# Row tiles in pairs, shifted copies on ScalarE, modulation sums later and a rank for the first row tile, in a two-layer hybrid mixer

## The chip, the cores and the metric

The kernel runs on one core of a Trainium2 chip. The metric is the device time of one execution in microseconds. Before the change it was run three times: 1634.55, 1635.33 and 1639.21 us, median 1635.33.

## What is computed

Two layers, each made of a SwiGLU feed-forward part, a token mixer and a second feed-forward part. Each part gets its input scaled and shifted by a modulation that is formed from a vector `c`, and ends in a residual sum and a layer norm. All data are float32; there are 256 tokens of 1024 channels.

```python
mod = (silu(c) @ ada_w[l] + ada_b[l]).reshape(3, 3, 1, D_MODEL)      # D_MODEL = 1024
u = modulate(h, mod[0, 0], mod[0, 1])
h = layer_norm(ALPHA * h + 0.5 * mod[0, 2] * swiglu_ffn(u, ...), ...)
u = modulate(h, mod[1, 0], mod[1, 1])
h = layer_norm(ALPHA * h + mod[1, 2] * hybrid_token_mixer(u, ...), ...)
u = modulate(h, mod[2, 0], mod[2, 1])
h = layer_norm(ALPHA * h + 0.5 * mod[2, 2] * swiglu_ffn(u, ...), ...)

def hybrid_token_mixer(u, ...):
    a_in, b_in, c_in, g_in = split(u @ w_in)
    y_a = silu(layer_norm(causal_dwconv(val * sigmoid(gate), width=31))) @ w_a_out
    y_b = rms_norm((ssd(silu(causal_dwconv(xbc, width=4))) + d * x) * silu(z)) @ w_b_out
    y_c = sparse_attention(c_in) @ w_c_out      # with compressed keys from overlapping blocks of 32
    g = sigmoid(g_in)
    return (g[0] * y_a + g[1] * y_b + g[2] * y_c) @ w_o
```

## The kernel before

**Layout.** Channels lie on the 128 partitions, so the 1024 channels are eight row tiles of 128 partitions x 256 tokens. All weights are cut into blocks of 128x128 and laid out in memory in the order in which they are used; eight blocks make a unit of 512 KB (`unit`, line 535). A unit is loaded into `raw`, ScalarE rounds it to the reduced precision of the fast matmul (`whi`), VectorE forms the rest (`wlo`), and each product is three matmuls: high by high, low by high, high by low (`triple`, lines 577 to 579; `pair` and `single`, lines 593 and 602). One weight tile is three matmuls of 256 columns.

**Order.** The program does not run as it is written. Every instruction is recorded with an engine, an estimated cost, its reads and writes, and a key (`rec`), and `schedule` (line 238) then lays all of them out: at each step, on each engine, the instruction that can start earliest by its estimate goes first; among equal starts the one with the lower key. The key is the number of the weight tile at which the step was recorded, unless `at(...)` or `key=` sets another: taps of the 31-wide convolution get keys spread between the tile of their input and a tile 670 after the start of `mix_a`; the halves of a weight unit get the unit's first tile less 20; a key under -9000 (`RUSH` is 20000) lets an engine wait for that step. TensorE and table-bound activations don't run more than 45 tiles ahead (`AHEAD`); VectorE isn't limited. The result is a fixed order for each engine, which the chip then runs with semaphores. SP issues all DMAs in one such order.

**Buffers.** The planner also gives out buffers. Eleven big ones of 8 KB per partition (`big8`) hold `uh`, `ul`, `ha`, `ca`, `mg`, `zs`, the gates, and each 1 MB block of modulation weights (`ada_raw`); they are given out in the order in which they are first used in the recorded program, first in first out. The 12 temporaries of 128x256 (`t256`, `TMP`), four 128x512 buffers (`pt`, shared by rope, attention and the exponentials of `ssd`) and six PSUM banks (`x_bank`) go to whoever comes first. Two PSUM banks (`mm_bank`) take turns under the weight products.

**Modulation sums.** `ada(l, t0, key)` loads two rows of 128 outputs (1 MB, issued with a key 30 tiles less) and forms each with one VectorE instruction over 1024 elements that multiplies by `sc` and accumulates; a small addition of the bias follows. In layer 0's mixer eight such steps are recorded by `side(i)` in five places, with `COUNT[i]` steps in the i-th; layer 1's mixer has none. Their results are read by `part_begin`, after the fourth row tile of `mix_out`, for the feed-forward part that follows.

**The mixer** (`mixer`, line 958), in recorded order, with the number of weight tiles: `early` (32), `mix_v` (32), `mix_small` (8), `mix_a` (96; input of the long convolution), `mix_c` (128; compression in `windows` and `compress`, rope, queries), gates `g2` (64), `mix_x` (128; short convolution), `attend` (beside the two before), `merge(0)` (64), `side(0)`, `mix_z` (64), `side(1)`, gates `g1` (64), `side(2)`, `ssd` (beside the two before) and `merge(1)` (64), `side(3)`, gates `g0` (64), `conv_end` (beside), `side(4)`, `merge(2)` (64), `mix_out` (64).

**At the start** the first feed-forward part takes its eight row tiles as they come: for each, `ready(k)` (in `start`, line 1558) issues the next loads, forms the modulation, `A`, and by `u_tile` the high part `uh`, a copy `u` and the low part `ul`.

Of the kernel before, what the change touches and what calls it, by code (L numbers as in the profile page):

```python
# [14 lines left out]
ALU = mybir.AluOpType  # L15
# [3 lines left out]
P = 128  # L19
# [333 lines left out]
COUNT = (2, 2, 2, 2, 0)  # L353
# [9 lines left out]
class Net(Plan):  # L363
    BIG = 11
    TMP = 12
# [60 lines left out]
    def x_bank(self, name="x", kind="misc"):  # L426
        return self.buf(self.pools["x"], "x", (P, 512), F32, name, kind=kind, psum=True)

# [670 lines left out]
    def windows(self, m, which):  # L1099
# [5 lines left out]
        for g in range(2):  # L1105
            r = slice(g * 64, g * 64 + 64)
            self.act(Sg[0:64, :, g, :], mv[r], AF.Copy)
            self.cp(Sg[64:, :, g, 0:T - 1], mv[r, :, 1:])
# [254 lines left out]
    def conv_end(self):  # L1363
# [12 lines left out]
        for e in range(KT):  # L1376
            with self.at(pos - TAIL[0] + TAIL[1] * e):
                self.tt(r[:, e], r[:, e], mean, ALU.subtract)
                sq.append(self.t256("sq"))
                self.act(sq[e], r[:, e], AF.Square)  # L1380
                if e % 4 == 3:
                    self.partial(var, sq[e - 3:], e > 3)
# [20 lines left out]
    def mix_x(self):  # L1403
# [9 lines left out]
        for i in range(16):  # L1413
# [7 lines left out]
            acc = self.t256("acc")  # L1421
# [7 lines left out]
            if i < 8:  # L1429
                tb = self.x_bank("xt")  # L1430
                for t in range(2):
                    self.trans(tb[:, t * P:t * P + P], o[:, t * P:t * P + P], self.c("ident"))
                for t in range(2):
                    self.tt(self.xdt[:, t, i * P:i * P + P].rearrange("p (h c) -> p h c", h=2),
                            tb[:, t * P:t * P + P].rearrange("p (h c) -> p h c", h=2),
                            self.smt[:, t, 64 + 2 * i:66 + 2 * i][:, :, None].to_broadcast([P, 2, 64]), ALU.mult)
            elif i >= 12:
                g = i - 12
                cb = self.x_bank("cb")
                self.mm(cb[:, :T], bc[:, g, :P], bc[:, 4 + g], True, True)  # L1440
                self.mm(cb[:, T:384], bc[:, g, P:], bc[:, 4 + g, P:], True, True)
                t = one((P, 384), f"cbt{g}")
                self.act(t, cb[:, :384], AF.Copy)
                self.cbt[g] = t

    def mix_z(self):
        self.zs = self.big8("zs")
        for i in range(0, KT, 2):
# [3 lines left out]
            for j in range(2):  # L1452
                zz = self.t256("zz")
                self.act(zz, m[:, j * T:j * T + T], AF.Copy, scale=0.5)
                th = self.t256("th")
                self.act(th, zz, AF.Tanh)
                self.stt(self.zs[:, i + j], th, 1.0, zz, ALU.add, ALU.mult)

    def ssd(self):
# [5 lines left out]
        for h in range(1, HEADS, 2):  # L1465
            with self.at(self.ssd0 + MARGIN[3] + (h - 1) * span / HEADS):
# [52 lines left out]
    def merge(self, step, yh, yl, rs=None, th=None):  # L1519
# [8 lines left out]
        for d in range(0, KT, 2):  # L1528
# [3 lines left out]
            for j in range(2):  # L1532
                y = m[:, j * T:j * T + T]
                t = gates[:, d + j]
                g = self.mg[:, d + j]
                if step == 0:
                    self.stt(g, t, 1.0, y, ALU.add, ALU.mult)
                    continue
                self.stt(t, t, 1.0, y, ALU.add, ALU.mult)
                if rs is not None:  # L1540
# [218 lines left out]
```

## Time and profile before

| | |
|---|---|
| median of three runs | 1635.33 us |
| profiled execution | 1632.52 us, its span 1630.7 us |
| TensorE busy, share of the span | 1580.8 us, 97% |
| weight loads | 1503.3 us, 92% |
| VectorE | 1381.3 us, 85% |
| ScalarE | 980.0 us, 60% |
| TensorE's mean granted clock | 0.995 |
| DMA, mean | 216 GB/s |
| TensorE in the chain that ended last | 84% |

The span is the time between the first and the last instruction of one execution. A busy engine isn't always the one that others wait for: the shares are means over stages. What a wait costs is read from TensorE's idle time and from what ended it.

### The profile page before, as it was taken

To read this page: it belongs to the slowest core of one execution; us is meant where nothing else is said; L and a number is where in the kernel's file an instruction comes from. 1 tells how busy PE (TensorE), PEld (TensorE's weight loads), DVE (VectorE), ACT (ScalarE), POOL (GpSimd) and SP (SyncE) were. 2 spreads that over 40 slices of the span, in tenths; PEclk is the share of its full clock that TensorE was granted. 3 is DMA by queue.
4 is the path that set the end of the run, shared out by engine and by line. 5 is a ranking of instruction groups with operands and counts; after the bars stand their busy time and mean duration, and the time that the engine had idled before them with its cause. 6 is when DMAs were issued, how large, how long until landed. Compare 5 with 4: busy or idle time off the path is not lost.

```text
span 1630.7 us, 33331 instructions
## 1 busy us (share of the span) xinstructions
PE 1580.8 (97%) x13228; PEld 1503.3 (92%) x13228; DVE 1381.3 (85%) x2676; ACT 980.0 (60%) x1810; POOL 8.3 (1%) x64
## 2 busy tenths in 40 slices
PE   7999999999999999999999999998999999999997
PEld 7999989889988888999989999998998898989996
DVE  7889789999999986899678885999999998776655
ACT  4644585588647466644475445845895567575443
POOL 0000000000000000000000000000000000000000
PEclk9999999999999999999999999999999999999998
DMA  9999665543276555899768885645332545657661
GB/s 372 320 342 396 226 215 180 176 130 98 92 279 214 173 175 187 300 346 364 253 234 294 320 302 174 230 161 173 124 109 92 178 154 161 194 191 241 222 197 42
DMA packets 89886, 351.86 MB, mean 216 GB/s; under 512 B 10369, under 2 KB 13697, under 8 KB 80130
## 3 DMA queue, kind: packets, MB, share of 16 engines
q1 hardware_dynamic: 89730, 349.73, 62.0%
q8 instruction: 104, 1.70, 0.4%
q14 instruction: 52, 0.43, 0.1%
HBM read 343.34 MB, written 1.05 MB: 211 GB/s over the span
## 4 chain that ended last, share of the span: by engine, by line
PE 84%; DVE 8%; DMA 3%; ACT 2%; issue 1%; SPq 0%; ACTq 0%; DVEq 0%
PE mm L577 15%; PE mm L578 15%; PE mm L579 15%; PE mm L455 3%; PE a L455 3%; PE a L593 2%; DMA ada<-in_ada 2%; PE g L577 2%; DVE wlo L474 2%; PE g L578 2%; PE g L579 2%; PE xb L577 2%; PE xb L578 2%; PE xb L579 2%; PE sb L1082 2%
## 5 line engine op out<-in xcount | busy, mean ns | idle before, releaser
L511 ACT ACTIVATE whi<-raw 128x1024 fp32r<-128x1024 f32 x470 | 496.8, 1059 | 315.9 <-PE mm L579 147.8
L474 DVE TENSOR_TENSOR wlo<-raw,whi 128x1024 fp32r<-128x1024 f32 x470 | 573.8, 1223 | 132.8 <-ACT whi L511 131.7
L577 PE MATMUL mm<-uh,whi 128*128 128x256 f32 x1392 | 384.8, 276 | 0.9 <-DVE h L474 0.9
L579 PE MATMUL mm<-ul,whi 128*128 128x256 f32 x1392 | 384.2, 276 | 0.0
L578 PE MATMUL mm<-uh,wlo 128*128 128x256 f32 x1392 | 384.2, 276 | 0.0
L577 PEld LDWEIGHTS mm<-uh,whi 128*128 128x128 f32 x1392 | 261.3, 188 | 2.5 <-ACT uh L511 1.2
L578 PEld LDWEIGHTS mm<-uh,wlo 128*128 128x128 f32 x1392 | 261.3, 188 | 0.1
L579 PEld LDWEIGHTS mm<-ul,whi 128*128 128x128 f32 x1392 | 261.3, 188 | 0.0
L577 PE MATMUL mm<-hh,whi 128*128 128x256 f32 x704 | 195.5, 278 | 0.0
L579 PE MATMUL mm<-hl,whi 128*128 128x256 f32 x704 | 194.7, 277 | 0.0
L578 PE MATMUL mm<-hh,wlo 128*128 128x256 f32 x704 | 194.7, 276 | 0.0
L493 DVE SCALAR_TENSOR_TENSOR ada<-ada,sc 128x1024 f32<-128x1024 f32 x144 | 173.7, 1223 | 24.8 <-DMA ada<-in_ada 19.3
L577 PEld LDWEIGHTS mm<-hh,whi 128*128 128x128 f32 x704 | 132.1, 188 | 1.3 <-issue 1.2
L579 PEld LDWEIGHTS mm<-hl,whi 128*128 128x128 f32 x704 | 132.3, 188 | 0.0
L578 PEld LDWEIGHTS mm<-hh,wlo 128*128 128x128 f32 x704 | 132.2, 188 | 0.1
L578 PE MATMUL g<-uh,wlo 128*128 128x256 f32 x384 | 108.2, 282 | 9.5 <-DVE wlo L474 9.5
L493 DVE SCALAR_TENSOR_TENSOR ca<-ap,vec,ca 128x256 f32<-128x256 f32 x240 | 115.1, 481 | 0.1
L577 PE MATMUL g<-uh,whi 128*128 128x256 f32 x384 | 113.8, 296 | 0.6 <-DVE g L493 0.6
L493 DVE SCALAR_TENSOR_TENSOR acc<-ap,vec,acc 128x256 f32<-128x256 f32 x224 | 108.1, 483 | 0.2
L579 PE MATMUL g<-ul,whi 128*128 128x256 f32 x384 | 107.3, 280 | 0.0
L511 ACT ACTIVATE sg<-mm 128x256 f32<-128x256 f32 x76 | 28.9, 381 | 91.8 <-PE mm L579 91.3
L578 PEld LDWEIGHTS g<-uh,wlo 128*128 128x128 f32 x384 | 73.0, 190 | 11.4 <-DVE wlo L474 11.2
(346 smaller groups left out, 3588.1 us busy)
## 6 DMA issues: line engine op xcount, KB each, us to landing
raw<-in_ws SPq DMA_DIRECT2D x498, 512.0 KB, 4.3
ada<-in_ada SPq DMA_DIRECT2D x71, 1024.0 KB, 8.0
w<-in_w SPq DMA_DIRECT2D x4, 1024.0 KB, 8.3
pt<-q SPq DMA_DIRECT2D x16, 128.0 KB, 5.0
ada<-in_ada SPq DMA_DIRECT2D x2, 512.0 KB, 4.6
x<-in_x SPq DMA_DIRECT2D x8, 128.0 KB, 10.8
pt<-kr SPq DMA_DIRECT2D x8, 128.0 KB, 2.2
kh<-kh SPq DMA_DIRECT2D x4, 256.0 KB, 4.3
```

Source lines behind the costliest of these rows:

```text
L455: return self.op("PE", cost, lambda: self.nc.tensor.matmul(real(out), lhsT=real(lhsT), rhs=real(rhs), start=start, stop=stop), [out], [lhs ...
L474: lambda: self.nc.vector.tensor_tensor(real(out), real(a), real(b), op), [out], [a, b], key)
L493: self.nc.vector.scalar_tensor_tensor(real(out), real(a), real(s), real(b), op0, op1, **k)
L511: self.nc.scalar.activation(real(out), real(a), f, **k)
L577: mm(o, lhsT=a, rhs=c, start=start, stop=False)
L578: mm(o, lhsT=b, rhs=c, start=False, stop=False)
L579: mm(o, lhsT=a, rhs=d, start=False, stop=stop)
L593: self.nc.tensor.matmul(o, lhsT=lhsT, rhs=rhs, start=first, stop=False)
L1082: self.nc.tensor.matmul(real(out), lhsT=real(lhsT), rhs=real(rhs), start=start, stop=stop)
```

## The change

1. `mix_x`, `mix_z`, `ssd`, `merge` and `conv_end` treat two row tiles in one instruction where they had one each (Tanh, the multiplications behind it, the gate products, the squares, the mean subtraction). In `mix_x` the taps of the short convolution accumulate straight in `xs` or `bc`. A single `th2` takes the place of temporaries for Tanh, the squares of a pair use the four `pt` buffers, and the temporaries go from 12 to 10.
2. In `windows` the two copies shifted by one token move from VectorE to ScalarE.
3. `COUNT` goes from (2, 2, 2, 2, 0) to (1, 1, 1, 2, 3).
4. In `start` the steps of row tile 0 get the key -20000 instead of -100.

```diff
-COUNT = (2, 2, 2, 2, 0)
+COUNT = (1, 1, 1, 2, 3)
-    TMP = 12
+    TMP = 10
+    def pair256(self, name):
+        return self.some((P, 512), "pt", 4).rearrange("p (a b) -> p a b", a=2)
+    def twice(self, v):
+        return v[:, None, :].to_broadcast([P, 2, T])
@@ windows
-            self.cp(Sg[64:, :, g, 0:T - 1], mv[r, :, 1:])
+            self.act(Sg[64:, :, g, 0:T - 1], mv[r, :, 1:], AF.Copy)
@@ conv_end
-        for e in range(KT):
-            with self.at(pos - TAIL[0] + TAIL[1] * e):
-                self.tt(r[:, e], r[:, e], mean, ALU.subtract)
-                sq.append(self.t256("sq"))
-                self.act(sq[e], r[:, e], AF.Square)
-                if e % 4 == 3:
-                    self.partial(var, sq[e - 3:], e > 3)
+        for e in range(0, KT, 2):
+            with self.at(pos - TAIL[0] + TAIL[1] * (e + 0.5)):
+                two = r[:, e:e + 2]
+                self.tt(two, two, self.twice(mean), ALU.subtract)
+                q = self.pair256("sq")
+                self.act(q, two, AF.Square)
+                sq += [q[:, 0], q[:, 1]]
+                if e % 4 == 2:
+                    self.partial(var, sq[e - 2:], e > 3)
@@ mix_x
-            acc = self.t256("acc")
+            o = self.xs[:, i] if i < 8 else bc[:, i - 8]
+            acc = o
...
-            th = self.t256("th")
-            self.act(th, acc, AF.Tanh)
-            o = self.xs[:, i] if i < 8 else bc[:, i - 8]
-            self.stt(o, th, 1.0, acc, ALU.add, ALU.mult)
+            if i % 2 == 0:
+                continue
+            th = self.one((P, 2, T), "th2")
+            both = self.xs[:, i - 1:i + 1] if i < 8 else bc[:, i - 9:i - 7]
+            self.act(th, both, AF.Tanh)
+            self.stt(both, th, 1.0, both, ALU.add, ALU.mult)
+            for i, o in ((i - 1, both[:, 0]), (i, both[:, 1])):
...
@@ mix_z
-            for j in range(2):
-                zz = self.t256("zz")
-                self.act(zz, m[:, j * T:j * T + T], AF.Copy, scale=0.5)
-                th = self.t256("th")
-                self.act(th, zz, AF.Tanh)
-                self.stt(self.zs[:, i + j], th, 1.0, zz, ALU.add, ALU.mult)
+            z = self.zs[:, i:i + 2]
+            self.act(z, m.rearrange("p (a b) -> p a b", a=2), AF.Copy, scale=0.5)
+            th = self.one((P, 2, T), "th2")
+            self.act(th, z, AF.Tanh)
+            self.stt(z, th, 1.0, z, ALU.add, ALU.mult)
@@ ssd
-                self.tt(x, x, self.zs[:, i], ALU.mult)
+                if i % 2 == 0:
+                    continue
+                x = self.xs[:, i - 1:i + 1]
+                self.tt(x, x, self.zs[:, i - 1:i + 1], ALU.mult)
                 if i % 4 == 3:
-                    sq = [self.t256("sq") for _ in range(4)]
-                    for g in range(4):
-                        self.act(sq[g], self.xs[:, i - 3 + g], AF.Square)
+                    sq = []
+                    for g in (i - 3, i - 1):
+                        q = self.pair256("sq")
+                        self.act(q, self.xs[:, g:g + 2], AF.Square)
+                        sq += [q[:, 0], q[:, 1]]
@@ merge (the loop over j is gone; y, t, g are pairs)
+            y = m.rearrange("p (a b) -> p a b", a=2)
+            two = slice(d, d + 2)
+            t, g = gates[:, two], self.mg[:, two]
...
+                self.tt(t, t, self.twice(rs), ALU.mult)
@@ start
-            self.ada(0, 8 + k, -100 + k, k, raws[k])
-            self.ts(A[:, k:k + 1], self.mod[0][:, 8 + k:9 + k], 1.0, None, ALU.add, key=-100 + k)
-            with self.at(-100 + k):
+            key = -100 + k if k else -RUSH
+            self.ada(0, 8 + k, key, k, raws[k])
+            self.ts(A[:, k:k + 1], self.mod[0][:, 8 + k:9 + k], 1.0, None, ALU.add, key=key)
+            with self.at(key):
```

## Rows read from the trace of the kernel before

**Rows 1.** The page, busy us (share of the span) xinstructions of each engine.

```profile
PE 1580.8 (97%) x13228; PEld 1503.3 (92%) x13228; DVE 1381.3 (85%) x2676; ACT 980.0 (60%) x1810; POOL 8.3 (1%) x64
```

**Rows 2.** Busy time by stage, layer 0's mixer: stretch, length, busy us of each engine.

```profile
213.34:433.70 220.36, 212.51 (x1810) 200.87 (x1811) 209.41 (x447) 163.85 (x376) 2.88 (x19) 1.00 0.47 154
...
525.00:551.00 26.00, 23.44 (x204) 22.34 (x200) 26.00 (x54) 10.45 (x12) 0.00 (x0) 1.00 0.59 203
551.00:580.00 29.00, 26.91 (x227) 23.72 (x227) 28.54 (x58) 20.73 (x34) 0.12 (x1) 1.00 0.53 170
580.00:607.00 27.00, 25.33 (x194) 24.55 (x195) 22.23 (x45) 16.79 (x32) 0.00 (x0) 0.94 0.53 170
```

**Rows 3.** The same for layer 1's mixer (PE, PEld, DVE, ACT, POOL; clock, DMA).

```profile
1021.64:1242.90 221.26, 214.03 (x1810) 202.46 (x1811) 209.42 (x447) 163.76 (x376) 2.17 (x13) 0.99 0.47 153
...
1334.20:1356.20 22.00, 22.00 (x198) 22.00 (x195) 18.27 (x30) 10.50 (x12) 0.00 (x0) 1.00 0.58 184
1356.20:1382.00 25.80, 25.80 (x235) 23.42 (x234) 20.42 (x39) 22.50 (x41) 0.00 (x0) 1.00 0.47 151
1382.00:1405.80 23.80, 22.12 (x195) 21.92 (x194) 19.52 (x35) 14.48 (x24) 0.00 (x0) 1.00 0.62 193
```

**Rows 4.** VectorE's groups, 200 to 640 us: xcount | busy, mean ns | idle before.

```profile
L493 DVE SCALAR_TENSOR_TENSOR ada<-ada,sc 128x1024 f32<-128x1024 f32 x16 | 19.3, 1233 | 0.0
...
L474 DVE TENSOR_TENSOR q<-q,cst 128x512 f32<-128x512 f32 x4 | 2.7, 686 | 0.0
```

**Rows 5.** VectorE's timeline: start us, us, instruction.

```profile
535.37 0.76 DVE L474 TENSOR_TENSOR g<-g,shift 128x256 f32<-128x256 f32 x2
...
556.67 0.45 DVE L474 TENSOR_TENSOR ca<-ca,acc 128x256 f32<-128x256 f32 x1
...
1334.65 0.42 DVE L474 TENSOR_TENSOR ca<-ca,acc 128x256 f32<-128x256 f32 x1
```

**Rows 6.** Waits of TensorE, layer 0's mixer: us in total, times, longest us.

```profile
PE g L578 <- DVE wlo L474: 4.9, 3, 2.9
PE mm L577 <- DVE g L493: 2.3, 1, 2.3
```

**Rows 7.** Waits of TensorE, layer 1's mixer.

```profile
PE g L578 <- DVE wlo L474: 4.6, 2, 2.9
...
PE mm L577 <- ACT g L511: 1.7, 1, 1.7
```

**Rows 8.** Busy time in five microseconds of layer 0's merge(2); 0.77 is the clock.

```profile
585.00:590.00 5.00, 5.00 (x36) 5.00 (x35) 2.92 (x8) 2.69 (x6) 0.00 (x0) 0.77 0.30 88
```

**Rows 9.** VectorE's groups from 525 to 557.2 us.

```profile
L493 DVE SCALAR_TENSOR_TENSOR ca<-ap,vec,ca 128x256 f32<-128x256 f32 x12 | 5.9, 489 | 0.0
L493 DVE SCALAR_TENSOR_TENSOR acc<-ap,vec,acc 128x256 f32<-128x256 f32 x11 | 5.5, 496 | 0.0
...
L493 DVE SCALAR_TENSOR_TENSOR g<-g,mm 128x256 f32<-128x256 f32 x7 | 2.7, 434 | 0.0
```

**Rows 10.** Instructions on the tile S: duration ns min/median/max.

```profile
L511 ACT ACTIVATE S<-kc x8: 592/594/598, 265.8 to 1081.1; 64x512 f32<-64x512 f32 x8
L506 DVE COPY S<-kc x8: 681/688/694, 266.4 to 1082.9; 64x510 f32<-64x510 f32 x8
```

**Rows 11.** The tile ada: time from issue to landing.

```profile
DMA to landing us min/median/max: 4.1/7.9/12.0
```

**Rows 12.** The timeline of the start: ScalarE's and TensorE's.

```profile
8.65 1.06 ACT L511 ACTIVATE whi<-raw 128x1024 fp32r<-128x1024 f32 x1 [2.02 <-DMA raw<-in_ws]
...
11.29 1.06 ACT L511 ACTIVATE whi<-raw 128x1024 fp32r<-128x1024 f32 x1 [1.58 <-DMA raw<-in_ws]
12.25 0.58 ACT L511 ACTIVATE u<-x,mod,A 128x256 f32<-128x256 f32 x1
...
12.74 0.59 ACT L511 ACTIVATE uh<-x,mod,A 128x256 fp32r<-128x256 f32 x1
...
13.38 0.58 PE L593 MATMUL a<-uh,whi 128*128 128x256 f32 x1 [7.39 <-ACT uh L511]
```

More of the change, by code (lines that the diff above doesn't have):

```diff
@@ L1424, in mix_x @@
                 self.stt(acc, xp[:, j:j + T], sw[:, i, j:j + 1], acc, ALU.mult, ALU.add)
-            th = self.t256("th")
-            self.act(th, acc, AF.Tanh)
-            o = self.xs[:, i] if i < 8 else bc[:, i - 8]
-            self.stt(o, th, 1.0, acc, ALU.add, ALU.mult)
[L1429 to L1444, printed above, removed]
+            if i % 2 == 0:
+                continue
@@ new lines, in mix_x @@
+            th = self.one((P, 2, T), "th2")
[3 more added lines that the diff above has]
+            for i, o in ((i - 1, both[:, 0]), (i, both[:, 1])):
+                if i < 8:
+                    tb = self.x_bank("xt")
+                    for t in range(2):
+                        self.trans(tb[:, t * P:t * P + P], o[:, t * P:t * P + P], self.c("ident"))
+                    for t in range(2):
+                        self.tt(self.xdt[:, t, i * P:i * P + P].rearrange("p (h c) -> p h c", h=2),
+                                tb[:, t * P:t * P + P].rearrange("p (h c) -> p h c", h=2),
+                                self.smt[:, t, 64 + 2 * i:66 + 2 * i][:, :, None].to_broadcast([P, 2, 64]), ALU.mult)
+                elif i >= 12:
+                    g = i - 12
+                    cb = self.x_bank("cb")
+                    self.mm(cb[:, :T], bc[:, g, :P], bc[:, 4 + g], True, True)
+                    self.mm(cb[:, T:384], bc[:, g, P:], bc[:, 4 + g, P:], True, True)
+                    t = one((P, 384), f"cbt{g}")
+                    self.act(t, cb[:, :384], AF.Copy)
+                    self.cbt[g] = t
@@ L1531, in merge @@
                 self.mm3(m[:, j * T:j * T + T], lambda k: yh[:, k], yl and (lambda k: yl[:, k]), KT)
[L1532 to L1540, printed above, removed]
-                    self.tt(t, t, rs, ALU.mult)
-                self.tt(g, g, t, ALU.add)
-                if step == 2 and 3 in NATIVE:
-                    self.act(g, g, AF.Copy, scale=0.5)
-                elif step == 2:
-                    self.act(self.mgh[:, d + j], g, AF.Copy, scale=0.5)
-                    self.stt(self.mgl[:, d + j], g, 0.5, self.mgh[:, d + j], ALU.mult, ALU.subtract)
+            y = m.rearrange("p (a b) -> p a b", a=2)
+            two = slice(d, d + 2)
+            t, g = gates[:, two], self.mg[:, two]
+            if step == 0:
+                self.stt(g, t, 1.0, y, ALU.add, ALU.mult)
+                continue
+            self.stt(t, t, 1.0, y, ALU.add, ALU.mult)
+            if rs is not None:
+                self.tt(t, t, self.twice(rs), ALU.mult)
+            self.tt(g, g, t, ALU.add)
+            if step == 2 and 3 in NATIVE:
+                self.act(g, g, AF.Copy, scale=0.5)
+            elif step == 2:
+                self.act(self.mgh[:, two], g, AF.Copy, scale=0.5)
+                self.stt(self.mgl[:, two], g, 0.5, self.mgh[:, two], ALU.mult, ALU.subtract)
     def mix_out(self, l):
```

## The prediction

> **What bounds the kernel now.** I read the page's busy totals first. TensorE is busy for 97% of the span [rows 1], so only its gaps can be won, and a shorter instruction on another engine is worth something only where TensorE waits for that engine. Next I asked for busy time by stage, with edges at the first matmul of each stage, for the mixer of layer 0 and for that of layer 1 [rows 2, 3]. Both layers do the same arithmetic, with one difference: layer 0 also forms sixteen modulation sums (`ada`, 19.3 us of VectorE [rows 4]). Layer 1 is thus a measurement, inside the same run, of what the mixer takes without them. From the value projection to the start of `merge(0)` layer 0 takes 220.4 us and layer 1 221.3. From there to `merge(1)` both take 91.3. Then they part: `merge(1)` takes 26.0 against 22.0 us, the gate stage 29.0 against 25.8, `merge(2)` 27.0 against 23.8. That is 10.4 us, or 9.5 after the lead of 0.9: the most that moving sums can give here.
>
> Why they part: in layer 0 VectorE has no idle time in `merge(1)` (26.00 of 26.00), in layer 1 it has 3.7 us (18.27 of 22.0). The last tap of the long convolution ends at 557.1 us in layer 0, 6 us after `merge(1)`, but at 1335.1 in layer 1, 21 us before its end [rows 5]. `conv_end` can't start without it, and `merge(2)` not without `conv_end`. In `merge(1)` TensorE also waits 2.3 us for a bank that VectorE hadn't emptied [rows 6], and after the gaps its clock was granted at 0.77 of full speed for 5 us [rows 8], which costs 1.15 us more.
>
> The waits by releaser [rows 6, 7] show the second place: in both layers TensorE waits for `wlo`, the low half of a weight block, during the gate stage before attention (4.9 and 4.6 us), in a stretch in which VectorE is busy all the time with rope, compression and convolution taps.
>
> **The change part by part.** All instructions keep their engine's order as the planner writes it, so a cheaper instruction first moves up what follows it; what it is worth depends on what it lets VectorE do sooner.
>
> *Pairs.* Two 128x256 operations back to back take 0.76 us [rows 5], one of 128x512 takes 0.686 [rows 4]: a pair saves 0.07 us. Per layer VectorE loses 8 instructions in `mix_x`, 4 each in `merge(0)`, `mix_z` and `ssd`, 12 in `merge(1)`, 12 in `merge(2)`, 4 in `conv_end`: 48 x 0.07 = 3.4 us, of which 1.4 before `merge(1)` and 0.8 in it. In `merge` the first half already waits for the second (one bank, one release), so pairing delays nobody there; in `mix_x` the even tile waits for the odd one's taps, and its readers (`xdt`, `cbt`) come a stage later. The single `th2` makes a Tanh wait for the VectorE step of the pair before; behind it on ScalarE stand the next weight halves. The pairs come one per bank, 16 blocks of matmuls apart, so I cost that at nothing.
>
> The Trainium skill ("Perfetto Trace Analysis", Optimizing Scalar/DVE Operations) puts the fixed part of a VectorE instruction at about 60 ns on SBUF and 125 ns on PSUM. Here the operation that reads PSUM (`g<-g,mm`, 434 ns [rows 9]) isn't longer than the ones beside it that don't. By the page's figure the 12 PSUM-fed pairs of a layer would save 0.06 us more each, 0.7 us a layer, and the forecast would be about 0.5 us lower.
>
> *Shifted copies.* Four copies a layer leave VectorE, 688 ns each [rows 10]: 2.75 us, some 30 us before the place where `wlo` is late. ScalarE does the like in 594 ns [rows 10], so four of them add 2.4 us to an engine that is 60% busy [rows 1]. Behind them in its queue stand weight halves (`whi`), for which VectorE waits and then TensorE. The cover is the lead of up to four blocks; if it were gone the cost would be 2.4 us a layer.
>
> *Where that goes.* The convolution has due times on the planner's line, and near 310 us its due times and those of `wlo` are about equal. With 2.75 us less before, some seven taps are already done and the rest are less urgent than `wlo`. Bounds for each layer: a gain of 2.75 us (less than the 4.9 and 4.6 us waited there), or a loss of 1.2 us, one 128x1024 operation, if the new order puts one more ahead. I take 1.3 each, nearer to nothing being lost: 2.6 us.
>
> *Sums later (`COUNT`).* Each issue is two operations of 1.233 us [rows 4], 2.47 us. Before, six of eight were due before the convolution's end, two in the gate stage. After: three, two, and three in `merge(2)`. By the buffers' first-in first-out order four ran before `merge(1)` and two in it; now three and none. So VectorE is relieved by 2.5 + 2.75 + 1.4 = 6.6 us before `merge(1)` and by 4.9 + 0.8 in it. The taps then left were 12 + 11, 11.4 us [rows 9]; 4.8 us remain, and layer 1's free 3.7 us and the 0.8 of the pairs hold 4.5. So the convolution ends close to the end of `merge(1)`, and the 9.5 us come back, less what the moved sums cost:
> - two in the gate stage: layer 1 has 25.8 - 20.4 = 5.4 us free there [rows 3] against 4.9. One may stand in front of the mean subtraction, on the path to `merge(2)`: 0 to 2.5, I take 1.0.
> - three in `merge(2)`, 7.4 us: free are 23.8 - 19.5 = 4.3, and 0.8 from pairs. 2.3 us spill over. `mix_out` has room, so 0 to 2.3; I take 1.5.
>
> Their DMAs (1 MB each) can be issued only once `yah` and `yal` have their buffers, in `merge(2)`; a landing takes 7.9 us (4.1 to 12.0 [rows 11]). The last sum is needed when `part_begin` makes A, 23.8 us of `merge(2)` and four of the eight row tiles of `mix_out` later [rows 3]: over 30 us, enough. Behind these DMAs on SP's queue stand weight blocks, six of which can be ahead. Net: 7.0 us, bounds 4.7 and 9.5.
>
> *First row tile ranked first.* ScalarE ran both weight halves, then `u`, then `uh`, for which TensorE waited until 13.38 us [rows 12]. The rank puts A and `u` sooner. But `uh` takes its buffer from the first-in first-out pool behind the third `ada` buffer, and a rank doesn't pass that; it stays behind the second weight half, without `u` in front: 12.74 - 12.25 = 0.5 us. Bounds: 0, and 2.6 if it came right behind the first half (9.71 + 0.59 and one `wlo` give about 10.8).
>
> *Ten temporaries.* Seven convolution accumulators hold a temporary each from 262 us on; of 12, five were left, now three. `mix_x`, `mix_z`, `ssd` and `conv_end` no longer take any, so the shortage is confined to compression and the first attention step. No row prices it: 0 to 2 us, taken as 0, as its users there come one after another. The squares share four `pt` buffers with `ssd`'s exponentials: nothing, they come once in four row tiles.
>
> *Layer 1's end.* 1.7 us are waited for the gate Tanh behind `conv_end`'s work on ScalarE [rows 7]; four instructions fewer there give 0.3.
>
> Sum: 7.0 + 2.6 + 0.5 + 0.3 = 10.4 us. The profiled execution took 1632.5 us with a span of 1630.7; the median of the runs is 1635.3, 2.8 above. Profiled: about 1622. Median: **1625 us**.
>
> **The rivals.**
> *More of it.* Both `wlo` places clear by 2.75 and layer 0 becomes layer 1: 9.5 + 5.5 + 2.6 + 0.3 = 17.9, 1617 us. For it: VectorE's saturation in both places. Against: the sums still have to run somewhere.
> *Half.* The sums' load only moves, all bounds on the poor side (4.7), and the new order gives nothing before attention: 4.7 + 0.5 = 5.2, 1630 us.
> *The change doesn't do it.* What VectorE saves is spent waiting, because layer 0's delay comes from the order of `conv_end` and not from the load; TensorE's stages stay as they are: 1634 us. Against it stands layer 1, with the same order.
> *Slower.* The planner's `dma` line takes 4.0 us for 1 MB (2.9 + 1.1) where the rows show 7.9. If it sets the three sums in `merge(2)` right behind their planned landing, VectorE stops there 4.0 us each, with `wlo` and the bank's release behind it: 12 us, 2.3 of spill, 1.15 for the clock, 15.5 in all, against 12.9 from the other parts: 1638 us. It turns the result from 3.2 us per sum on; at the longest landing (12.0) it would be 1650. Against it: the sums' due times are 20 tiles apart, so they needn't stand right behind the landing.
>
> **How the numbers follow.** Forecast 0.58, more 0.10, half 0.16, nothing 0.09, slower 0.07. The forecast spreads over its bounds, 1619 to 1631. The range 1616 to 1633 takes in most of "more" and "half" and leaves out about 2 in 10. A difference of 0.3%, 4.9 us, is about what can be told from no change. Faster than 1630.4: nearly all of the forecast, all of "more" and over half of "half", 0.77. Within: the rest of these, "nothing" and nearly half of "slower", 0.19. Slower: 0.04.
>
> **What would show it.** The three stages of layer 0 should take about 22.5, 26.5 and 25 us, and the last tap should end before 552 us. The waits for `wlo` before attention should be near 3.5 us a layer. The first weight matmul should start near 12.9. Wrong would be: waits of VectorE for `ada` DMAs in `merge(2)` over 3 us each, a last tap that hardly moved, or new waits for `wlo` around the shifted copies.

## The result, and the profile after

Nineteen runs of each kernel on the same chips: the changed kernel takes 1627.53 us in the median, the kernel before 1638.78; the ratio is 0.9939, with a 95% interval of 0.9926 to 0.9952. Forecast were 1625 us and a range of 1616 to 1633, from a kernel before of 1635.3; the difference is 11.3 us, forecast 10.4. The sum of the steps came out, but not by the steps: two of them were wrong by about as much, in opposite directions, and the experiments are about these two.

The profiled execution took 1627.53 us, its span 1625.7. That is only 5 us less than the profiled execution of before, which lies at the fast end of its kernel's runs (1631 to 1644). The feed-forward parts differ from run to run: the first, from the first weight matmul to its last, took 183.0 to 188.6 us over the kernels below in which it does the same work, and 4.3 us of that are a slower pace of TensorE that the clock doesn't show (last section), not transfers. The mixers' stages repeat better (e5 below), so the comparison goes by them; a lower clock or the slower pace moves even those by some 2 us.

The page's busy totals of the changed kernel, which answer [rows 1]: VectorE loses 104 instructions and 10.7 us, TensorE stays at 97%.

```profile
PE 1583.2 (97%) x13228; PEld 1507.3 (93%) x13228; DVE 1370.6 (84%) x2572; ACT 981.3 (60%) x1762; POOL 8.3 (1%) x64
```

Busy time by stage in layer 0's mixer, edges at the first matmul of each stage, those of the gate stage and of the end at the last matmul before (value projection to `merge(1)`; then `merge(1)`, gate stage, `merge(2)`, `mix_out`), as in [rows 2]: stretch, length, PE, PEld, DVE, ACT, POOL, clock, DMA share, GB/s.

```profile
212.47:521.83 309.36, 304.40 (x2482) 282.84 (x2482) 293.74 (x609) 214.26 (x464) 4.06 (x27) 0.99 0.52 168
521.83:543.76 21.93, 21.93 (x197) 21.93 (x194) 21.27 (x34) 10.29 (x11) 0.00 (x0) 1.00 0.62 214
543.76:569.83 26.07, 26.07 (x236) 23.33 (x236) 24.59 (x42) 19.89 (x31) 0.12 (x1) 1.00 0.51 168
569.83:598.57 28.74, 25.45 (x195) 24.45 (x194) 26.46 (x50) 16.45 (x28) 0.00 (x0) 0.94 0.70 252
598.57:623.46 24.89, 24.13 (x203) 22.62 (x202) 16.13 (x26) 12.63 (x18) 0.00 (x0) 1.00 0.61 183
```

The same for layer 1, as in [rows 3]; the two stages between are left out, they are as before.

```profile
1019.33:1328.29 308.96, 305.08 (x2481) 283.28 (x2481) 293.85 (x608) 214.22 (x464) 2.37 (x15) 0.99 0.47 154
...
1376.09:1400.83 24.74, 22.81 (x194) 22.62 (x193) 19.43 (x26) 14.29 (x22) 0.00 (x0) 1.00 0.61 188
1400.83:1424.26 23.43, 23.43 (x203) 22.89 (x202) 13.85 (x20) 12.03 (x17) 0.00 (x0) 1.00 0.58 180
```

Against before, by the same edges (there 311.65, 25.67, 29.30, 26.85 and 23.07 us in layer 0, and 312.56, 21.94, 25.86, 23.71 and 22.60 in layer 1):

| part | forecast, us | this profile | a second profile (e5) |
|---|---|---|---|
| first weight matmul | -0.5 | -1.1 | -0.9 |
| value projection to `merge(1)`, both layers | -2.6 | -5.9 | -7.8 |
| `merge(1)` and gate stage, layer 0 | -6.0 | -7.0 | -7.0 |
| `merge(2)`, layer 0 | -2.0 | +1.9 | +1.9 |
| `mix_out`, layer 0 | 0 to +2.3 | +1.8 | +1.9 |
| `merge(1)` to `mix_out`, layer 1 | -0.3 | +1.9 | +1.9 |
| sum of these parts | -10.4 in all | -8.4 | -10.0 |

The last tap of the long convolution, which ended at 557.1 us [rows 5], now ends at 546.2, 2.4 us after `merge(1)` (VectorE's timeline: start, us):

```profile
545.76 0.43 DVE L480 TENSOR_TENSOR ca<-ca,acc 128x256 f32<-128x256 f32 x1
```

In layer 1 it ends 21 us before the end of `merge(1)` (first line below). `conv_end` begins with means over all row tiles, and TensorE's last matmuls for them, in layer 0 and then in layer 1, start 19.5 and 23.7 us before `merge(2)`:

```profile
1328.71 0.42 DVE L480 TENSOR_TENSOR ca<-ca,acc 128x256 f32<-128x256 f32 x1
```

```profile
550.37 0.59 PE L461 MATMUL st<-cmb,mean 128*128 128x256 f32 x2
...
1352.42 0.59 PE L461 MATMUL st<-cmb,mean 128*128 128x256 f32 x2
```

What TensorE waits for in layer 0 (total, times, longest): first up to `merge(1)`, then from there to the end of `mix_out`. `wlo` stood at 4.9 us [rows 6], the bank that VectorE hadn't emptied at 2.3; that one is gone. Waits for ScalarE in `merge(2)` were there before, 2.3 us for `yah` and 0.4 for the Tanh `g`; now they are 1.1 and 2.0. A line of the kernel before, then the changed one:

```profile
PE mm L577 <- ACT yah L511: 2.3, 2, 1.3
```

```profile
PE g L584 <- DVE wlo L480: 2.8, 1, 2.8
...
PE mm L583 <- ACT g L517: 2.0, 1, 2.0
PE mm L583 <- ACT yah L517: 1.1, 2, 0.7
PE mm L585 <- DVE mgl L499: 0.4, 2, 0.2
```

And in layer 1's mixer, the answer to [rows 7] (the two longest):

```profile
PE g L584 <- DVE wlo L480: 2.4, 1, 2.4
PE mm L583 <- ACT g L517: 1.9, 1, 1.9
```

Fifteen microseconds around the start of layer 0's `merge(2)`, in fives (columns as above). ScalarE has no pause for ten of them, TensorE idles, and its granted clock then falls to 0.66; [rows 8] showed 0.77 at the like place.

```profile
565.00:570.00 5.00, 5.00 (x47) 5.00 (x46) 4.92 (x13) 5.00 (x12) 0.00 (x0) 1.00 0.50 168
570.00:575.00 5.00, 2.79 (x15) 1.79 (x14) 4.02 (x12) 5.00 (x14) 0.00 (x0) 1.00 0.99 409
575.00:580.00 5.00, 3.92 (x20) 3.92 (x21) 5.00 (x10) 2.70 (x6) 0.00 (x0) 0.66 0.94 390
```

The start, ScalarE's timeline and TensorE's first weight matmul, against [rows 12]: `u` now runs between the two weight halves, `uh` still behind both.

```profile
8.90 1.06 ACT L517 ACTIVATE whi<-raw 128x1024 fp32r<-128x1024 f32 x1 [2.25 <-DMA raw<-in_ws]
9.86 0.58 ACT L517 ACTIVATE u<-x,mod,A 128x256 f32<-128x256 f32 x1
10.66 1.06 ACT L517 ACTIVATE whi<-raw 128x1024 fp32r<-128x1024 f32 x1 [0.22 <-DMA raw<-in_ws]
11.63 0.58 ACT L517 ACTIVATE uh<-x,mod,A 128x256 fp32r<-128x256 f32 x1
...
12.27 0.58 PE L599 MATMUL a<-uh,whi 128*128 128x256 f32 x1 [6.25 <-ACT uh L517]
```

### The profile page after: what moved, and what is told of

It reads as the page before. It is cut to its first block, busy times and chain, and to the rows that moved or that the text cites. A ratio compares the mean times of both kernels' runs of the same rounds, so it can differ in the third digit from the quotient of the medians.

```text
span 1625.7 us, 33200 instructions
## 1 busy us (share of the span) xinstructions
PE 1583.2 (97%) x13228; PEld 1507.3 (93%) x13228; DVE 1370.6 (84%) x2572; ACT 981.3 (60%) x1762; POOL 8.3 (1%) x64
## 5 line engine op out<-in xcount | busy, mean ns | idle before, releaser
L583 PEld LDWEIGHTS g<-uh,whi 128*128 128x128 f32 x384 | 73.6, 192 | 6.6 <-issue 6.2
## 6 DMA issues: line engine op xcount, KB each, us to landing
x<-in_x SPq DMA_DIRECT2D x8, 128.0 KB, 10.8
```

The costliest lines, as they stand in the source:

```text
L583: mm(o, lhsT=a, rhs=c, start=start, stop=False)
```

## The experiments

Ratios are against the kernel before, run beside each on the same chip; they aren't the plain quotients of the medians. "v to merge(1)" is the length from the value projection to `merge(1)`, "merge(1) to mix_out" that of the four stages behind it, both by the edges above; the first number is layer 0's.

| kernel | median, us | ratio (95% interval) | v to merge(1) | merge(1) to mix_out |
|---|---|---|---|---|
| before | 1637 to 1640 | 1 | 311.7 / 312.6 | 104.9 / 94.1 |
| changed | 1627.53 | 0.9939 (0.9926 to 0.9952) | 309.4 / 309.0 | 101.6 / 96.0 |
| e1 sums' places alone | 1637.17 | 0.9979 (0.9956 to 1.0002) | 311.8 / 313.1 | 100.7 / 95.7 |
| e2 changed, old places | 1630.39 | 0.9940 (0.9920 to 0.9960) | 308.9 / 309.0 | 104.1 / 96.0 |
| e3 copies alone | 1634.02 | 0.9957 (0.9929 to 0.9985) | 310.7 / 310.5 | 103.8 / 94.1 |
| e4 pairs alone | 1637.16 | 0.9997 (0.9968 to 1.0025) | 313.1 / 313.4 | 101.6 / 94.4 |
| e5 changed, again | 1631.53 | 0.9949 (0.9927 to 0.9971) | 308.2 / 308.2 | 101.7 / 96.0 |
| e6 three sums to the first part | 1625.17 | 0.9907 (0.9876 to 0.9939) | 309.4 / 307.5 | 100.7 / 94.4 |
| e7 all eight sums to the first part | 1628.89 | 0.9934 (0.9909 to 0.9959) | 308.2 / 309.6 | 96.0 / 96.0 |
| e8 ten temporaries alone | 1641.68 | 1.0023 (0.9998 to 1.0049) | 314.8 / 311.9 | 104.2 / 98.2 |
| e9 Tanh first, later request | 1629.01 | 0.9950 (0.9931 to 0.9968) | 307.7 / 309.9 | 103.5 / 97.0 |
| e10 the same, five sums moved | 1627.51 | 0.9942 (0.9924 to 0.9960) | 310.0 / 311.2 | 101.5 / 98.2 |
| e11 eleven temporaries | 1670.87 | 1.0197 (1.0177 to 1.0217) | see below | see below |
| e12 e6 with less on ScalarE | 1618.98 | 0.9893 (0.9866 to 0.9920) | 309.3 / 310.2 | 98.5 / 94.1 |

### The parts one by one (e1 to e4, e8)

e1, the kernel before with the sums' new places:

```diff
-COUNT = (2, 2, 2, 2, 0)
+COUNT = (1, 1, 1, 2, 3)
```

> The kernel before with the new places of the modulation sums and nothing else. Theory (load): the delay of layer 0's conv_end is the load that VectorE carries before it; this alone takes 7.4 us of sums out of VectorE's way before the end of merge(1), less than the 11.4 us of taps and 8 of pairs and copies together, so the convolution should end near 549 us and the run should be some 5 us shorter than the kernel before (1633 against 1639, on the medians of the second set of runs). Rival (all parts together): without the 3.4 us of the pairs and the 2.75 of the copies the taps still end after merge(1), and what is gained there is spent in merge(2): 0 to 2 us. Rival (order): the gap is set by the order of conv_end, the taps may end earlier but the stages of TensorE stay: 0.

e2, the changed kernel with the sums' old places (the same two lines, the other way round):

> The changed kernel with the sums in their old places, (2, 2, 2, 2, 0). Theory (load): pairs, copies and the rank alone give 3 to 5 us against the kernel before; the sums' 5 to 7 us are missing. Layer 0's merge(1) should take 25 us or so again and the gate stage 28, while merge(2) falls back below 27. Rival (pairs and copies carry it): VectorE gets 3.4 + 2.75 us in each layer from them, enough to end the convolution in time with the sums in either place: then this is within 2 us of the changed kernel.

e3, the kernel before with the shifted copies on ScalarE:

```diff
-            self.cp(Sg[64:, :, g, 0:T - 1], mv[r, :, 1:])
+            self.act(Sg[64:, :, g, 0:T - 1], mv[r, :, 1:], AF.Copy)
```

> The kernel before with the four shifted copies of each layer on ScalarE and nothing else. Theory: what VectorE has less, 2.75 us a layer some 30 us before the gate stage, lets wlo come sooner; the wait of TensorE for wlo in that stage falls from 4.9 and 4.6 us to about 3.5 in each layer, and the run gets 2 to 3 us shorter. Rival (ScalarE): whi is late behind the copies and the gain is eaten: waits for whi or wlo of 1 to 2 us near 280 and 1100 us and no change in the time. Rival (order): the taps simply move up, wlo waits as long as before: no change before attention, but up to 2.7 us in layer 0's merge(1).

e4, the changed kernel with the lines of e1, e3 and the rank at the start put back, so that only the pairs and the ten temporaries are left:

> The kernel before with pairs, the short convolution accumulating in place, one buffer for Tanh and ten temporaries, and nothing else. Theory: 3.4 us of VectorE's time a layer, of which 1.4 before merge(1) and 0.8 in it help layer 0 (about 2 us of the 9.5), 0.3 at layer 1's end; temporaries cost nothing: 2 us shorter, or 0 if the planner's order spends it. Rival (temporaries): ten instead of twelve hold up compression or the first attention step, TensorE shows new waits between 240 and 310 us and between 1050 and 1115: the run is 0 to 2 us longer.

e8, the kernel before with fewer temporaries:

```diff
-    TMP = 12
+    TMP = 10
```

> The kernel before with ten temporaries of 128x256 instead of twelve and nothing else. The pairs alone had lost 1.5 us in layer 0 and 1.1 us in layer 1 between the value projection and the first gates against the kernel before. Theory (temporaries): that is the price of two temporaries fewer, and shows here too: 1 to 2 us more in that stretch in each layer, longer waits for wlo. Rival (order): it comes from the planner's other order with the pairs, and here that stretch stays within 0.5 us.

Measured: the sums' places alone shorten the four stages of layer 0 by 4.2 us, the pairs alone by 3.3 (104.89 to 101.55); together with the copies, in the changed kernel, it is 3.3. Counted from the start of `merge(1)`, the last tap ends 6.8 us sooner by the sums alone, 1.2 by the pairs alone and 7.8 in the changed kernel: the convolution's end gains the sum of the two, TensorE's stages don't. Putting the sums back (e2) lengthens these stages by 2.5 us, and the whole run by an amount that the intervals can't tell from nothing. So the forecast 7.0 us for the sums were too many by about half.

The copies are worth more than was put down. TensorE's wait for `wlo` before attention in layer 0 of e3, with the copies moved, and the stretch from the value projection to `merge(1)` before, in e3 and in e8 (length, then what TensorE is busy of it):

```profile
PE g L578 <- DVE wlo L474: 2.7, 1, 2.7
```

```profile
213.34:524.99 311.65, 303.80 (x2482) 281.37 (x2482) 297.05 (x631) 212.91 (x480) 4.08 (x27) 1.00 0.52 173
...
212.53:523.19 310.66, 305.66 (x2481) 283.35 (x2481) 294.33 (x627) 215.34 (x484) 4.06 (x27) 0.99 0.50 174
...
215.01:529.83 314.82, 306.70 (x2482) 283.61 (x2482) 297.50 (x631) 213.26 (x480) 4.05 (x27) 0.99 0.49 171
```

The wait is 4.1 us in e4 and in e8; layer 1 shows 2.7 in e3, 4.0 and 4.0. The copies take 2.2 and 1.9 us off the wait, against 1.3 in the forecast, and 2.9 us off TensorE's idle time in layer 0's stretch (7.9 to 5.0); 1.9 of these go again to a TensorE that is busy for longer with the same matmuls, at a lower clock (0.99) and pace. The rival of late `whi` behind the copies didn't show: no wait for `whi` is among them. Ten temporaries alone make the stretch 3.2 us longer in layer 0 and 0.7 shorter in layer 1. In layer 0 TensorE's idle time there is only 0.3 us more (8.1); the other 2.9 are time in which it is busy, at a lower clock (0.99 against 1.00) and pace again, so a cost of the temporaries isn't shown, and the run's interval (0.9998 to 1.0049) doesn't show one either. The same holds for the 1.4 and 0.8 us by which e4's stretch is longer: its idle time is 0.7 and 0.3 less than before. With the copies gone from VectorE (e2), the wait is 2.6 and 2.7 us and the stretch is 1.5 to 1.8 us shorter than in e3, some 1.0 of it idle time.

### What repeats (e5)

The changed kernel, unchanged.

> The changed kernel once more, unchanged, to see which of its stages repeat. In the first profile the two feed-forward parts between the mixers lost 3.7 us against the kernel before (a stop of 3.98 us of VectorE for a modulation block near 954 us), and merge(2) with mix_out of layer 0 lost 3.7. Theory: the mixer's stages are set by the written order and repeat within 1 us, the cost of 3 to 4 us in merge(2) and mix_out too; what the feed-forward parts lost is the transfers' chance and comes elsewhere or not at all. Rival: the stop near 954 us belongs to the changed order and comes again at the same place with over 3 us.

`merge(1)`, gate stage, `merge(2)` and `mix_out` of layer 0 took 21.93, 26.07, 28.73 and 24.93 us, all within 0.04 of the first profile, and TensorE's idle time in `merge(2)` is 3.3 us in both; that the lengths agree so closely is partly luck, as the clock was 0.88 there now and 0.94 in the first. The stretch before differs by 1.1 us. The parts between the mixers took 375.7 us against 379.4 and 375.3 before: the stop near 954 us didn't come again with over 3 us (TensorE's wait there was 1.4 us now, 3.1 in the first).

### What makes merge(2) long (e6, e7)

e6:

```diff
-SPLITA = 48
-COUNT = (1, 1, 1, 2, 3)
+SPLITA = 54
+COUNT = (1, 1, 1, 2, 0)
```

> The changed kernel with the three steps of layer 0's merge(2) formed in the first feed-forward part instead. Theory (the three sums cost 3 to 4 us in merge(2) and mix_out): merge(2) of layer 0 falls from 28.8 to about 25 us and mix_out from 24.9 to 23.4, and VectorE and the transfers have room for three more in the first feed-forward part (64.9 of 73.7 us and 68.0 of 83.0 busy, transfers 0.92 and 0.76), so the run is 2 to 4 us shorter than the changed kernel. Rival (transfers): the first feed-forward part is bound by its transfers, 3 MB more at about 0.33 MB per us cost up to 9 us there, and the run is up to 5 us longer.

e7 has `SPLITA = 64`, so nothing is left for the mixer.

> The changed kernel with all eight steps of layer 0's mixer formed in the first feed-forward part: layer 0's mixer then has no sums at all and is what layer 1's is, which tests the ceiling of 9.5 us. If that ceiling holds, the stages from merge(1) to mix_out of layer 0 take what layer 1's take (22.0, 25.8, 24.8 and 23.4 us, against 21.9, 26.1, 28.8 and 24.9 of the changed kernel): 5 to 6 us shorter there. The first feed-forward part gets 8 MB more and 19.7 us more of VectorE: it should get longer by 5 to 20 us, so the run as a whole is longer than the changed kernel unless the transfers there have room that the shares (0.92 and 0.76) hide. Rival: the stages stay longer than layer 1's without any sums, so the sums were not what parted the layers.

Layer 0's `merge(2)` and `mix_out` in e6, then its four stages in e7 (columns as above):

```profile
571.56:601.14 29.58, 26.38 (x194) 25.36 (x193) 21.49 (x33) 16.75 (x29) 0.00 (x0) 0.88 0.47 157
601.14:624.21 23.07, 23.07 (x203) 22.52 (x202) 14.40 (x20) 12.38 (x17) 0.00 (x0) 1.00 0.54 183
```

```profile
530.37:552.31 21.94, 21.94 (x197) 21.94 (x194) 17.89 (x20) 10.51 (x12) 0.12 (x1) 1.00 0.55 192
552.31:578.17 25.86, 25.86 (x235) 23.48 (x235) 19.76 (x32) 21.98 (x36) 0.00 (x0) 1.00 0.41 144
578.17:603.78 25.61, 23.68 (x195) 23.48 (x193) 19.42 (x26) 14.31 (x22) 0.00 (x0) 0.93 0.54 184
603.78:626.37 22.59, 22.59 (x203) 22.05 (x202) 14.27 (x20) 12.38 (x17) 0.00 (x0) 1.00 0.57 188
```

My expectation for e6 fell where it mattered. With no sums in it at all `merge(2)` still takes 29.6 us, and TensorE idles there for 3.2 us as in the changed kernel. Nor are the transfers what stops it: at the start of `merge(2)` they fill 0.99 and 0.94 of two slices in the changed kernel, and 0.31 and 0.29 in e6. What the three sums cost stands one stage later: `mix_out` goes from 24.9 to 23.1, 1.8 us, because the last two of their instructions run on VectorE ahead of the last `mg` and `mgl`, for which `mix_out` waits (the `mgl` row above). The room in the first feed-forward part was there: 185.4 us in e6 lies inside 183.0 to 188.6. e7 gives the ceiling: 104.9 - 96.0 = 8.9 us, against 9.5 read from layer 1. There the last tap ends as early as in layer 1 (47 us before `merge(2)`; 23.6 in e6 as in the changed kernel), the waits for `yah` are gone and only the 1.9 us for the Tanh are left, as in layer 1. So what layer 0's `merge(2)` loses to layer 1's hangs on where the convolution ends. But with eight more blocks the first feed-forward part takes 193.4 us, 4.8 to 10.4 more than where it is the same work, with 6.0 us of new waits of TensorE, and the 5.6 us that layer 0's mixer gains on the changed kernel are gone again.

### ScalarE: order or load (e9, e10, e12)

In the changed kernel the last Tanh of the gates stands behind some twenty instructions of `conv_end` on ScalarE, and TensorE waits 2.0 us for it. e9 puts it first, and also tests what held `uh` at the start:

```diff
-            self.act(g[:, i:i + 2], m.rearrange("p (a b) -> p a b", a=2), AF.Tanh, scale=0.5)
+            self.act(g[:, i:i + 2], m.rearrange("p (a b) -> p a b", a=2), AF.Tanh, scale=0.5,
+                     key=self.tile_no - RUSH if name == "g0" and i == KT - 2 else None)
@@ start, ready(k)
-            if k + NRAW < KT:
+            if k + NRAW < KT and k:
                 raw(k + NRAW)
...
                 self.u_tile(k, self.x[:, k], A[:, k:k + 1], self.mod[0][:, k:k + 1])
+            if k == 0:
+                raw(NRAW)
```

> The changed kernel with two edits at two places. (1) The last Tanh of the gates g0 gets a key that lets ScalarE wait for it, in both layers. In layer 0 of the changed kernel that Tanh ran at 575.45 us, 5.5 us after the bank that it empties was full, behind twenty instructions of conv_end, and TensorE waited 1.96 us for it in merge(2) (1.93 in layer 1) and had its clock at 0.66 for 5 us after. Theory (ScalarE's order is what is late next): the wait goes, merge(2) takes 2 to 3.5 us less in layer 0 (28.7 before) and 1 to 2.5 less in layer 1 (24.7 to 25.6), 3 to 5 us in all. Rival (the chain of conv_end): TensorE waits for yah and yal at the same place instead, merge(2) keeps its length within 0.7 us. (2) At the start the third modulation block of the first feed-forward part is asked for after the first row tile's steps are recorded, so that uh no longer stands behind it in the order of the big buffers. Theory (order of the buffers): uh runs right behind the first weight half, and the first weight matmul starts near 10.8 us, not 12.3. Rival: it stays above 12, and the buffers were not what held uh. The later stages of the first feed-forward part are bound by transfers and may take the gain back.

TensorE's waits in layer 1's `merge(2)` in e9:

```profile
PE mm L583 <- ACT whi L517: 1.7, 1, 1.7
PE mm L584 <- DVE wlo L480: 0.9, 1, 0.9
```

The wait for the Tanh is gone, and one for the next weight half stands in its place: whatever comes last in ScalarE's queue is what is late. `merge(2)` takes 29.2 us in layer 0 and 26.7 in layer 1, longer than without the edit, and layer 0's gate stage is 1.2 us longer too; the waits of both stages there add up to 3.4 us where they were 3.3. So a better place for the Tanh isn't enough. The start came out as the order of the buffers says: ScalarE's timeline and the first weight matmul of e9.

```profile
8.68 1.06 ACT L517 ACTIVATE whi<-raw 128x1024 fp32r<-128x1024 f32 x1 [1.97 <-DMA raw<-in_ws]
9.65 0.58 ACT L517 ACTIVATE uh<-x,mod,A 128x256 fp32r<-128x256 f32 x1
...
10.29 0.58 PE L599 MATMUL a<-uh,whi 128*128 128x256 f32 x1 [4.20 <-ACT uh L517]
```

e10 has both edits of e9 and `SPLITA = 58`, `COUNT = (1, 1, 1, 0, 0)`.

> The same two edits, and five of the eight steps of layer 0's mixer formed in the first feed-forward part; the other three come one each before merge(1), as in the changed kernel. Theory: without the two sums in the gate stage conv_end ends 3 to 5 us earlier against TensorE, so merge(2) of layer 0 falls to about 24 us and mix_out to 22.6; with the first feed-forward part 2 to 3 us longer for 5 MB more, the run is 6 to 9 us shorter than the changed kernel (about 1622 against 1630). Rival (transfers): the first feed-forward part takes what the mixer gives, as with all eight (193 us against 183 to 189): no better than the version that moved three.

It missed: `merge(2)` took 30.9 us in layer 0 and 27.3 in layer 1, so taking the two sums out of the gate stage didn't shorten it. The three sums that stand before the convolution's end are still there, and the last tap ends 23.6 us before `merge(2)` as in the changed kernel. The Tanh put first is in this kernel too, so the two edits can't be told apart.

e12 is e6 with the start of e9, without its Tanh, and with less work for ScalarE:

```diff
-                self.act(x, x, AF.Identity, bias=gb[:, 8 + k:9 + k], scale=gb[:, k:k + 1])
+                if k % 2:
+                    self.ts(x, x, gb[:, k:k + 1], gb[:, 8 + k:9 + k], ALU.mult, ALU.add)
+                else:
+                    self.act(x, x, AF.Identity, bias=gb[:, 8 + k:9 + k], scale=gb[:, k:k + 1])
```

> The version that forms three more steps in the first feed-forward part, with the later request of the third modulation block at the start, and with the scale and shift of every second row tile in conv_end on VectorE instead of ScalarE (four instructions a layer). Theory (what is late next in merge(2) is ScalarE's load: it is busy without a pause from 565 to 575 us, with 24 instructions of conv_end between the last weight halves): 4 x 0.49 = 2 us less on ScalarE give back 1.5 to 3 us of merge(2) in layer 0 (29.6 without this edit, its waits and the lower clock after them included) and up to 1.5 in layer 1 (24.0), first weight matmul near 10.3 us, the run 2 to 5 us shorter than the 1625 of the version without. Rival (latency): the steps of one row tile follow each other from engine to engine, and it is this chain and not the load that is late; then the waits for yah stay and merge(2) stays within 0.7 us, or gets longer, as VectorE is 4.5 to 4.7 of 5 us busy there as well.

Around the start of layer 0's `merge(2)`, in fives, and TensorE's waits there: e6, then e12, with e12's `merge(2)` as a whole first (e6's is above).

```profile
570.00:575.00 5.00, 4.10 (x30) 3.41 (x28) 4.48 (x14) 5.00 (x15) 0.00 (x0) 1.00 0.31 105
575.00:580.00 5.00, 2.70 (x13) 2.37 (x12) 4.02 (x8) 4.32 (x9) 0.00 (x0) 0.63 0.29 103
...
PE mm L583 <- ACT g L517: 2.3, 1, 2.3
PE mm L583 <- ACT yah L517: 0.9, 2, 0.7
```

```profile
570.53:597.60 27.07, 24.60 (x194) 24.21 (x193) 22.45 (x34) 15.26 (x23) 0.00 (x0) 0.94 0.54 174
...
570.00:575.00 5.00, 2.53 (x21) 2.14 (x19) 5.00 (x11) 4.97 (x11) 0.00 (x0) 1.00 0.32 94
575.00:580.00 5.00, 5.00 (x30) 5.00 (x31) 4.08 (x10) 1.83 (x5) 0.00 (x0) 0.66 0.46 152
...
PE mm L584 <- DVE wlo L480: 1.7, 1, 1.7
PE mm L583 <- ACT g L517: 0.7, 1, 0.7
```

`merge(2)` falls from 29.58 to 27.07 us in layer 0, and from 23.97 to 23.75 in layer 1. In the five microseconds after 575 ScalarE is busy for 1.83, where it was 4.32; before them VectorE is now the one without a pause (5.00 of 5.00), and its `wlo` comes last. TensorE's idle time in `merge(2)` falls from 3.2 to 2.5 us in layer 0 and from 1.9 to 1.0 in layer 1; the rest of the 2.5 us in layer 0 is its clock, 0.88 and 0.94. So where the convolution ends this late, ScalarE's load is what holds `merge(2)`, and VectorE's comes right behind; this rests on one profile of each. With 1618.98 us, ratio 0.9893, e12 is faster than the kernel before, and its interval lies below the changed kernel's; it overlaps with that of e6.

### Eleven temporaries (e11)

```diff
-    TMP = 10
+    TMP = 11
-            "pad" tile of 48 floats, "unit" in a buffer of its own
+            "pad" tile of 32 floats, "unit" in a temporary
```

> The changed kernel with eleven temporaries of 128x256 instead of ten; the room comes from a small constant at the start that takes a temporary, and from 64 bytes of padding. Theory (temporaries): two fewer had cost the kernel before 2.4 us in layer 0 between the value projection and mix_x, so one more gives back about 1 us there (144.65 and 143.32 us in two runs of the changed kernel) and the run is 0 to 2 us shorter. Rival: with the copies gone from VectorE and three sums fewer ahead, ten are enough and that stretch stays within 0.7 us.

It tells nothing of temporaries: the run is 2% longer than before, and all stages of its mixers but one are longer than the changed kernel's (the last section shows it). Whether an eleventh would help is open.

## Why the prediction was right, and where it wasn't

*What bounds the kernel, and the ceiling.* Held. Layer 1 as a measurement of layer 0 without sums gave 9.5 us, e7 8.9.

*Sums later, 7.0 us.* The first half of the step held: `merge(1)` and the gate stage fell to 21.9 and 26.1 us (forecast 22.5 and 26.5) and the last tap ended before 552. The step that failed is the sentence by which "the 9.5 us come back, less what the moved sums cost": it gave `merge(2)` 25 us, and it took 28.7. A convolution that "ends close to the end of `merge(1)`" isn't layer 1's, which ends 21 us ahead of that end: here it ended 2.4 us behind it, `conv_end`'s means came 4.2 us later against `merge(2)` than in layer 1, and TensorE, there 7 us sooner, met `conv_end`'s last part, with ScalarE at 5.00 of 5.00. It idled 3.3 us in `merge(2)`, against 1.9 in layer 1, and its clock fell. In e7, where the last tap ends as in layer 1, it idles 1.9; e12 shows that ScalarE's load sets part of the rest. The stop and the lower clock after it were already in `merge(2)` before (a clock of 0.77 in [rows 8], 2.3 us for `yah`) and I counted them as won. The sums' own spill was sized well: 1.5 us forecast, 1.8 measured, one stage later than put. Instead of 7.0 the four stages gave 3.3, below the bound of 4.7, and the pairs are in that too.

*`wlo` before attention, 2.6 us.* Right in kind, too small: the wait fell from 4.9 and 4.6 us to 2.8 and 2.4 (forecast 3.5), by the copies nearly alone (e3), and pairs, with the ten temporaries, gave 1.5 to 1.8 us a layer more in that stretch once the copies were gone (e2 against e3). Going by the waits, the copies were put at some 60% of what they gave, and the pairs at nothing in this place. Measured for the stretch, both layers: 5.9 and 7.8 us. The two errors, -3.7 and +3.3 to +5.2, cancel: that the total lies 2.5 us from the forecast is partly luck.

*Pairs at nothing in the way, temporaries at nothing.* Held as far as tested. The pairs weren't in the way: with them e2's stretch is shorter than e3's. For the temporaries nothing speaks against the 0, as TensorE's idle time hardly moves in e8, but no run has the change with twelve, so their price in its company isn't measured.

*First row tile, 0.5 us.* 1.1 and 0.9, of which 0.5 by the order as worked out; in this profile the second weight block also landed sooner (ScalarE began on it at 10.66 us, not 11.29). The reason given, that `uh` stands behind the third modulation buffer, is shown by e9: 10.29 us without it, against the bound of 10.8.

*Layer 1's end, 0.3 us gained.* Wrong: 1.9 lost. The wait for the Tanh went from 1.7 to 1.9, and TensorE ran slower afterwards (below). That differs between profiles of one kernel: the clock fell in e5 and not in the first. Kernels that kept clock and pace there (e3, e4, e6, e12) took 94.1 to 94.4 us, with 94.4 for e4 and e6, which have the pairs: so 0.3 us lost is the change's own part, and no gain.

*The rivals.* "Slower" named stops of VectorE for modulation blocks in `merge(2)`; none came. "Half" was nearest in its mechanism for the sums (4.7 at the poor end, 3.3 came), but its second half, nothing before attention, was wrong. "The change doesn't do it" fell with the last tap at 546 us.

The Trainium skill ("Perfetto Trace Analysis", Optimizing Scalar/DVE Operations) gave a larger fixed part for VectorE instructions that read PSUM. VectorE's groups from 525 to 557.2 us of the changed kernel have one that reads PSUM (`mm`) and others of the same size that don't, such as:

```profile
L480 DVE TENSOR_TENSOR g<-g,shift 128x512 f32<-128x512 f32 x4 | 2.8, 694 | 0.0
L499 DVE SCALAR_TENSOR_TENSOR g<-g,mm 128x512 f32<-128x512 f32 x4 | 2.8, 688 | 0.0
```

No such difference shows here, 688 against 694 ns, so nothing here bears out the 0.5 us by that figure.

## What to carry to other kernels

When an engine's load before a deadline is cut, ask for every stage behind it what the bottleneck engine meets when it arrives sooner, and read the busy share of the other engines in five-microsecond slices there: an engine at 60% over the run was at 100% in the ten microseconds that counted. Two parts of a change that relieve the same deadline needn't add up on the bottleneck engine (4.2 and 3.3 us alone, 3.3 together), and a part that gives nothing alone (the pairs before attention) can give beside another, so price them together. When a wait only moves to the next releaser as its instruction is put first, suspect the load rather than the order. Before a stage that got longer or shorter is put down to an edit, compare the bottleneck engine's idle time and its time per instruction apart.

## What the hardware showed

TensorE has two paces that the granted clock doesn't tell apart. From start to start its 128x256 matmuls came 113.3 ns apart in most long stretches without waits, and 117.7 ns apart in others. In the first feed-forward part of e1, e2 and e5 some 960 matmuls had the slower pace, 4.3 us in all; before, in the changed kernel's first profile and in e3 almost none had it. The same work of the changed kernel, 60 to 135 us, first profile and then e5, with the clock at 1.00 in both:

```profile
L585 PE MATMUL mm<-ul,whi 128*128 128x256 f32 x222 | 61.3, 276 | 0.0
```

```profile
L585 PE MATMUL mm<-ul,whi 128*128 128x256 f32 x212 | 59.6, 281 | 0.0
```

The slower pace also came for some tens of microseconds after some of the stops in `merge(2)`. The groups of one matmul line in layer 1's `merge(2)`, 1384 to 1400 us, in the two profiles of the changed kernel (first, then e5), with the clock at 1.00 in the first:

```profile
L585 PE MATMUL mm<-yal,whi 128*128 128x256 f32 x46 | 12.9, 281 | 0.0
```

```profile
L585 PE MATMUL mm<-yal,whi 128*128 128x256 f32 x48 | 13.3, 276 | 0.0
```

In e5 the clock fell to 0.83 for two slices of five microseconds and the pace was the full one after. In the first it never showed a fall, and the matmuls stayed 281 ns long. The two stages took 48.2 us either way, 1.9 more than before.

In e11 that slower pace holds from the first stage to the last. A feed-forward stretch of e11, 655 to 765 us, without a wait; in the changed kernel the mean there is 276 ns:

```profile
L585 PE MATMUL mm<-ul,whi 128*128 128x256 f32 x296 | 83.3, 281 | 0.0
```

Five nanoseconds of some 113 on each of 13,228 matmuls come to 66 us at most; 42 are what it lost against e9, beside which it ran. What e11 alters for TensorE is where its operands lie in memory (64 bytes of padding and 512 of a constant are gone in front of them) and, through the eleventh temporary, the planned order. That the addresses did it is possible but not shown: no run changed them alone, and the pace came elsewhere without such an edit. What selects it is open.
